# Fewer and wider small products on TensorE in a gated-DeltaNet decoder step, and another last stage

## The chip, the cores and the metric

The kernel runs on one core of a Trainium2 chip, in one launch. The metric is the device time of that launch in microseconds (us). Five engines work beside each other and wait for one another through semaphores: PE (TensorE: matmuls and transposes, results into PSUM), ACT (ScalarE), DVE (VectorE), POOL (GpSimd) and SP (SyncE, which here issues every DMA). A profile of one execution names each instruction with its engine, start, duration, output and inputs.

## What is computed

One inference step of a trunk of two layers, in fp32, over 512 prompt tokens and 64 sample tokens (8 sequences of 8 tokens), which share all weights. Layer 0 is a pooling mixer, layer 1 a gated DeltaNet mixer; each is followed by a SwiGLU feed-forward block, all with RMS norms before and after. The part that the change touches is the DeltaNet mixer and the very end:

```python
proj = h @ w_in
qkv_c, new_conv = short_conv(qkv, conv_buf, conv_w)   # width 4; conv_buf: 3 earlier rows per sample
q = l2norm(qkv_c[q part]) * 128 ** -0.5               # 8 heads of 128
k = l2norm(qkv_c[k part])                             # 8 heads of 128
v = qkv_c[v part]                                     # 16 heads of 128
o, s_new = gated_delta_chunked(q, k, v, g, beta, s0)  # exact delta rule, chunk by chunk
o = rms_norm(o, o_norm) * silu(z)
y = o @ w_out
...
x = x + rms_norm(swiglu(h, ffn_w_in[1], ffn_w_out[1]), norm_ffn_post[1])   # the last line: y_prompt, y_sample
```

`new_conv` (the last three rows before the convolution, for the prompt and for each sample) and the states are outputs too.

## The kernel before

**Layout.** Activations lie with channels on the 128 partitions and tokens along the free dimension (512 prompt columns, then 64 sample columns). Every dense product is made from three fp32r products (`mm3`): each operand is split into a high and a low part (`wh`, `wl` for weights; `hH`, `hL` or `aH`, `aL` for activations), and high times high, high times low and low times high are summed in PSUM. ACT makes the high part of a weight tile, DVE or POOL the low part (tiles `wraw`, `wh`, `wl`, three buffers each).

**The DeltaNet mixer** runs in four groups G of two key heads and four value heads. `project(G)` computes the group's eight 128-channel chunks (two of k, two of q, four of v; PSUM tile `ps_m`), convolves them on DVE and turns them to token-major by `finish`. `core(G)` computes the delta rule of the prompt (`inv32`, `scan`) and of the samples (`sample_front`, `sample_heads`). The program writes `core(G)` ahead of `project(G+1)`, and the two overlap.

The pieces that the change touches:

- *Convolution states.* For each half of a group (four chunks) the 24 stored rows (8 samples by 3) of each chunk are loaded into `crow` with 24 rows on partitions and four chunks side by side (lines 1807 to 1813), and each chunk is transposed on its own (1814, 1815). On the way out the 27 new rows of each chunk (`nct`: 3 of the prompt, 24 of the samples) are transposed one chunk at a time (1920 to 1922), copied by ACT to `nco` (which shares the one buffer of `crow`), and stored by two DMAs for each run of neighbouring chunks (1925 to 1929).
- *Norms of the samples.* The sample columns of q and k (tile `qks`, each written twice so that 128 columns are filled) are squared by DVE or POOL into `sqs` (1911, 1912). Four fp32 products with a column of ones sum the squares over the channels (1848 to 1850). The prompt's norms come from ACT squares with a running sum (`ksq`). A second product in `sample_front` brings the samples' k to token-major (`pt`, 1980), from which `ks` is made.
- *Outputs of the samples.* `TQ` holds, for two heads each, `T` in its upper 64 partitions and `Q` in partitions 64 to 127, columns 0 to 63. The output product uses one 64 by 64 corner of the array (`tile_position=(64, 64)`, 2075 to 2078). `gate_s` transposes the four heads' outputs, 64 partitions by 128 (2281 to 2287).
- *The end.* In the last block of the second feed-forward part, tokens are handled in two pieces, `LAST`: 320 and then 256 columns. Each finished chunk `yo` is squared by ACT into `nsq` and added to `nacc` (`add_sq`); `turn_y` scales it and transposes it into PSUM (`ps_B`) or, for the first four chunks of a piece, on into SBUF (`yT`). `finish1` (2454) sums `nacc` over the channels by products with ones (`ps_n`), takes the root on ACT and the reciprocal on DVE (`nrc`), and adds the scaled result to the residual (`xa`, `xb`) with four DVE instructions for the last 256 tokens, two per 128 rows. Three DMAs store these rows.

PSUM banks are used in rings (1154): `x` is one bank, through which go all transposes of `project`, `finish` and the gates; `k` has two.

**The order.** No engine runs the program in the order in which it is written. A class `Plan` records every operation, estimates its cost, places all operations with a list scheduler by priority, then moves priorities at random in windows of the schedule. The random moves to make are given by a table of seeds, `CHOSEN` (eight passes, 7,451 seeds); the operations are issued in the resulting order on each engine, SP's DMAs included. `EITHER` marks operations that the planner may give to DVE or POOL. Where PE would stand idle for long, the plan fills in products of ones (`ps_w`).

All operations are issued from two lines (785, and 781 for the fillers), so the rows of the profile are told apart by tile names.

Of the kernel before, what the change touches and what calls it, by code (L numbers as in the profile page):

```python
# [11 lines left out]
F32 = mybir.dt.float32  # L12
# [36 lines left out]
CW = 4  # L49
# [11 lines left out]
class Plan:  # L61
# [2446 lines left out]
```

## Time and profile before

| | us |
|---|---|
| three runs, median (lowest to highest) | 1501.12 (1500.25 to 1501.59) |
| the profiled execution, its own time | 1501.94 |
| the profiled execution, span from first to last instruction | 1500.2 |
| PE busy | 1476.1 |
| DVE busy | 1128.9 |
| ACT busy | 841.3 |
| POOL busy | 124.7 |

The span is shorter than the time of the same execution by 1.7 us. The DeltaNet mixer lies between 480 and 1035 us from the span's start, which is where the tiles `crow`, `nct`, `sqs`, `TQ` and `vs` appear; the last feed-forward block ends at 1489 us. A row of the timeline gives start, duration, engine, line, operation, output and inputs, and how many equal instructions are merged in it. PE's instructions overlap one another, so the slot of one product is the distance between starts, not its duration.

### The profile page before, as it was taken

How to read it: one execution, taken by the hardware profiler on the slowest of the kernel's cores; microseconds unless marked ns; L12 is line 12 of the kernel's file. 1: busy time of each engine (PE TensorE's matmuls, PEld its weight loads, DVE VectorE, ACT ScalarE, POOL GpSimd, SP SyncE). 2: the span in 40 equal slices, each digit the busy share in tenths (PEclk: the TensorE clock that was granted, in tenths of full speed). 3: DMA queues.
4: the chain of work that ended last, by engine and by line, in shares of the span. 5: the costliest groups of instructions: out<-in, count | busy, mean ns of one | idle time of the engine just before them, and what ended most of it. 6: DMA issues, size and time to landing. Idle time of an engine off the chain costs nothing.

```text
span 1500.2 us, 30095 instructions
## 1 busy us (share of the span) xinstructions
PE 1476.1 (98%) x11734; PEld 1433.4 (96%) x11734; DVE 1128.9 (75%) x2273; ACT 841.3 (56%) x1824; POOL 124.7 (8%) x258
## 2 busy tenths in 40 slices
PE   8999999999999999999999999999999999999997
PEld 8999999999999899898999899899999999999997
DVE  7994566778678797995997899567797566767855
ACT  7754443435455866865775775555474443534544
POOL 5200000000012111100220110000110000000000
PEclk9999999999999999999999999999999999999998
DMA  7643323233456433434344434746753323224162
GB/s 200 182 131 92 104 78 105 71 114 89 136 149 165 123 97 99 121 101 133 104 125 138 120 111 139 216 141 204 216 173 107 106 80 89 87 87 121 57 185 88
DMA packets 322821, 186.96 MB, mean 125 GB/s; under 512 B 13163, under 2 KB 315596, under 8 KB 322671
## 3 DMA queue, kind: packets, MB, share of 16 engines
q1 hardware_dynamic: 322679, 185.04, 42.6%
q8 instruction: 92, 1.51, 0.4%
q14 instruction: 50, 0.41, 0.1%
HBM read 154.72 MB, written 30.52 MB: 123 GB/s over the span
## 4 chain that ended last, share of the span: by engine, by line
PE 87%; DVE 7%; ACT 2%; DMA 2%; issue 1%; POOL 0%; DVEq 0%; SPq 0%; POOLq 0%; ACTq 0%
PE ps_A L785 27%; PE ps_B L785 27%; PE ps_m L785 19%; PE ps_s L785 5%; PE ps_k L785 4%; PE ps_x L785 2%; PE ps_e L785 1%; DVE wl L785 1%; DVE ac L785 1%; DVE nacc L785 1%; PE ps_n L785 1%; DMA og<-og_d 1%; DVE y L785 1%; PE ps_g L785 0%; DVE vt L785 0%
## 5 line engine op out<-in xcount | busy, mean ns | idle before, releaser
L785 ACT ACTIVATE wh<-wraw 128x1024 fp32r<-128x1024 f32 (+4 forms) x214 | 208.1, 973 | 174.8 <-PE ps_A L785 78.2
L785 DVE TENSOR_TENSOR wl<-wraw,wh 128x1024 fp32r<-128x1024 f32 (+4 forms) x214 | 238.8, 1116 | 76.4 <-ACT wh L785 70.0
L785 PE MATMUL ps_m<-hH,wh 128*128 128x320 f32 (+1 forms) x832 | 251.1, 311 | 0.0
L785 PE MATMUL ps_m<-hL,wh 128*128 128x320 f32 (+1 forms) x832 | 249.1, 308 | 0.0
L785 PE MATMUL ps_m<-hH,wl 128*128 128x320 f32 (+1 forms) x832 | 246.4, 308 | 0.0
L785 PEld LDWEIGHTS ps_m<-hH,wh 128*128 128x128 f32 x832 | 155.3, 189 | 4.8 <-issue 1.2
L785 PEld LDWEIGHTS ps_m<-hL,wh 128*128 128x128 f32 x832 | 155.3, 189 | 1.7 <-issue 0.6
L785 PEld LDWEIGHTS ps_m<-hH,wl 128*128 128x128 f32 x832 | 154.6, 189 | 1.8 <-issue 0.6
L785 PE MATMUL ps_B<-hL,wh 128*128 128x288 f32 (+2 forms) x420 | 124.1, 304 | 0.4 <-POOL hL L785 0.4
L785 PE MATMUL ps_B<-hH,wh 128*128 128x288 f32 (+2 forms) x420 | 122.8, 305 | 0.6 <-ACT hH L785 0.6
L785 PE MATMUL ps_B<-hH,wl 128*128 128x288 f32 (+2 forms) x420 | 123.1, 304 | 0.0
L785 PE MATMUL ps_A<-aL,wh 128*128 128x288 f32 (+2 forms) x408 | 116.4, 297 | 0.0
L785 PE MATMUL ps_A<-aH,wl 128*128 128x288 f32 (+2 forms) x408 | 116.0, 297 | 0.0
L785 PE MATMUL ps_A<-aH,wh 128*128 128x288 f32 (+2 forms) x408 | 115.6, 298 | 0.0
L785 PE MATMUL ps_A<-hH,wl 128*128 128x288 f32 (+2 forms) x396 | 110.4, 289 | 0.3 <-DVE wl L785 0.3
L785 PE MATMUL ps_A<-hL,wh 128*128 128x288 f32 (+2 forms) x396 | 110.3, 288 | 0.0
L785 PE MATMUL ps_A<-hH,wh 128*128 128x288 f32 (+2 forms) x396 | 110.1, 290 | 0.2 <-ACT nsq L785 0.2
L785 PE MATMUL ps_B<-aL,wh 128*128 128x288 f32 x296 | 82.9, 295 | 0.0
L785 PE MATMUL ps_B<-aH,wl 128*128 128x288 f32 x296 | 82.7, 295 | 0.0
L785 PE MATMUL ps_B<-aH,wh 128*128 128x288 f32 x296 | 82.7, 295 | 0.0
L785 DVE SCALAR_TENSOR_TENSOR ac<-u,cwt,ac 128x600 f32<-128x600 f32 x96 | 79.3, 837 | 1.5 <-ACT ac L785 1.0
L785 PEld LDWEIGHTS ps_B<-hL,wh 128*128 128x128 f32 x420 | 78.1, 188 | 0.9 <-POOL hL L785 0.9
(459 smaller groups left out, 4029.9 us busy)
## 6 DMA issues: line engine op xcount, KB each, us to landing
wraw<-in_ffn_w_in_dram SPq DMA_DIRECT2D x64, 512.0 KB
wraw<-in_gdn_w_in_dram SPq DMA_DIRECT2D x53, 512.0 KB
graw<-in_ffn_w_in_dram SPq DMA_DIRECT2D x36, 512.0 KB
wraw<-in_ffn_w_out_dram SPq DMA_DIRECT2D x26, 448.0 KB
wraw<-in_gdn_w_out_dram SPq DMA_DIRECT2D x21, 512.0 KB
wraw<-in_ffn_w_out_dram SPq DMA_DIRECT2D x32, 320.0 KB
St<-in_state_gdn_rec_dram SPq DMA_DIRECT2D x32, 256.0 KB
out_dram<-St SPq DMA_DIRECT2D x32, 256.0 KB
```

The lines of the kernel that those rows point to most:

```text
L785: calls[e](*a, **k)
```

## The change

Five edits, and a new table of seeds.

1. *Convolution states.* The rows of four chunks are stacked on 96 partitions (8 DMAs of 24 rows per group instead of 3), so that one transpose does what four did; on the way out, four chunks of 27 rows are transposed at once to 108 partitions, copied by ACT as 108 by 128 instead of 27 by 512, and stored by 16 DMAs per group instead of 6.
2. *Norms of the samples.* The products of `sqs` with ones go, and so do the squares by DVE or POOL. Instead the samples' q and k are transposed (`pt`, one per chunk, in ring `x`), and ACT squares them with a running sum into a fifth column of `ksq`. The same transpose of k gives `ks`, so that the product `pt` in `sample_front` goes; `ks` gets two buffers.
3. *Outputs of the samples.* `Q` moves to columns 64 to 127 of `TQ`, and the output product takes the whole of `TQ` and of `vn` (with zeros in its upper half, set by POOL). `gate_s` transposes all 128 partitions.
4. *The last sums.* In the last piece the square of the last chunk is no longer added to `nacc` by DVE: both tiles go through products with ones into one PSUM sum.
5. *The last adds and stores.* The pieces are taken in reverse; for the last 128 rows one half is scaled by ACT and added by POOL; and each 512-column half is stored by itself, with six DMAs instead of three.

`CHOSEN` keeps eight passes and holds 5,709 other seeds, so the order of every engine's instructions is drawn anew.

```diff
@@ out(), last block of the feed-forward part
-                add_sq(tp, s["acc"], yc, i, hf)
+                if ends and hf.i == 1 and i == NC - 1:
+                    s["acc"].append(halftile(tp, "nsq", hf, 2))
+                    ACT.activation(s["acc"][1], yc, AF.Square)
+                else:
+                    add_sq(tp, s["acc"], yc, i, hf)
@@ project()
-            sqs = pp.tile([P, 4, P], F32, name="sqs", tag="sqs", bufs=1)
+            ks = gp.tile([P, 2, P], F32R, name="ks", tag="ks", bufs=2)
...
-                crow = pp.tile([R0 + CW - 1, 4, P], F32, name="crow", tag="crow", bufs=1)[:R0]
+                crow = pp.tile([P, P], F32, name="crow", tag="crow", bufs=1)[:4 * R0]
                 for _, c, k in (r for r in runs if r[0] == j4):
                     c0 = chunks[4 * j4 + c][2] * P
-                    SP.dma_start(crow[:, c:c + k], state_gdn_conv[0].rearrange("b r d -> (b r) d")[:, c0:c0 + k * P]
-                                 .rearrange("r (c p) -> r c p", c=k))
-                for c in range(4):
-                    PE.transpose(cp[:, 4 * j4 + c], crow[:, c], ident[:R0, :R0])
+                    for i in range(k):
+                        SP.dma_start(crow[(c + i) * R0:(c + i + 1) * R0],
+                                     state_gdn_conv[0].rearrange("b r d -> (b r) d")[:, c0 + i * P:c0 + (i + 1) * P])
+                PE.transpose(cp[:, 4 * j4:4 * j4 + 4].rearrange("p c r -> p (c r)"), crow, ident[:4 * R0, :4 * R0])
@@ finish(), kind "k"
+                    pt = bank("x")[:, :P]
+                    PE.transpose(pt, qks[:, i, :2].rearrange("p x t -> p (x t)"), ident)
+                    ACT.activation(u[:, SEQ:], pt, AF.Square, accum_out=ksq[:, SPANS, i:i + 1])
+                    ACT.activation(ks[:, i], pt, AF.Copy)
+                    DVE.tensor_tensor(ks[SMP:, i], pt[SMP:], ks[SMP:, i].bitcast(F32), op=sub)
@@ finish(), kind "q"
+                    pt = bank("x")[:, :P]
+                    PE.transpose(pt, qks[:, i, 1:].rearrange("p x t -> p (x t)"), ident)
+                    ACT.activation(u[:, SEQ:], pt, AF.Square, accum_out=ksq[:, SPANS, 2 + i:3 + i])
-                        pst = bank("x")[:, :4]
-                        for c in range(4):
-                            PE.matmul(pst[:, c:c + 1], sqs[:, c], ones[:, 0:1], start=True, stop=True)
-                        DVE.tensor_scalar(vt_[:, 0, :SPANS], ksq, EPS, None, op0=add)
-                        DVE.tensor_scalar(vt_[:, 0, SPANS], pst, EPS, None, op0=add)
+                        DVE.tensor_scalar(vt_[:, 0], ksq, EPS, None, op0=add)
@@ project(), per chunk and at its end
-                if kind != "v":
-                    EITHER.tensor_tensor(sqs[:, j].rearrange("p (x t) -> p x t", x=2), dup(dss), dup(dss), op=mult)
...
-                pn_ = bank("x", (P, 4, P))[:R]
-                for c in range(4):
-                    PE.transpose(pn_[:, c], nct[:, 4 * j4 + c], ident)
-                nco = pp.tile([R, 4, P], F32, name="nco", tag="crow", bufs=1)
+                pn_ = bank("x")[:4 * R, :P]
+                PE.transpose(pn_, nct[:, 4 * j4:4 * j4 + 4].rearrange("p c r -> p (c r)"), ident)
+                nco = pp.tile([P, P], F32, name="nco", tag="crow", bufs=1)[:4 * R]
                 ACT.activation(nco, pn_, AF.Copy)
-                    for dst, src in ((nc_prompt[0, 0], nco[:CW - 1]),
-                                     (nc_sample[0].rearrange("b r d -> (b r) d"), nco[CW - 1:])):
-                        SP.dma_start(dst[:, cols].rearrange("r (c p) -> r c p", c=k), src[:, c:c + k])
+                    for i in range(k):
+                        c0, r = (chunks[4 * j4 + c][2] + i) * P, (c + i) * R
+                        SP.dma_start(nc_prompt[0, 0, :, c0:c0 + P], nco[r:r + CW - 1])
+                        SP.dma_start(nc_sample[0].rearrange("b r d -> (b r) d")[:, c0:c0 + P], nco[r + CW - 1:r + R])
@@ sample_front()
-                PE.matmul(pt, kk, ident, start=True, stop=True)
...
-                ACT.activation(ks[:, hd], pt, AF.Copy)
-                DVE.tensor_tensor(ks[E2[1], hd], pt[E2[1]], ks[E2[1], hd].bitcast(F32), op=sub)
@@ sample_heads()
+                POOL.memset(vn[lo], 0.0)
...
-                DVE.tensor_tensor(vn, pv[:, 0].rearrange("p (e v) -> p e v", e=2),
-                                  bet[:, SPANS, h2].unsqueeze(2).to_broadcast([P, 2, P]), op=mult)
+                DVE.tensor_tensor(vn[up], pv[up, 0].rearrange("p (e v) -> p e v", e=2),
+                                  bet[up, SPANS, h2].unsqueeze(2).to_broadcast([SMP, 2, P]), op=mult)
...
-                    PE.matmul(po[up, 0, e * P:(e + 1) * P], Qs[:, hd, e], vn[up, e], start=True, stop=True,
-                              tile_position=(SMP, SMP))
+                    PE.matmul(po[:, 0, e * P:(e + 1) * P], TQ[:, hd, e], vn[:, e], start=True, stop=True)
@@ gate_s()
-            po = bank("x")[:, :4 * SMP].rearrange("p (h t) -> p h t", h=4)
+            po = bank("x", (P, 4, P))
             for h in range(4):
-                PE.transpose(po[:, h], o[:, h], ident[up, up])
+                PE.transpose(po[:, h], pr_[3][:, h], ident)
@@ finish1()
+            for j, a in enumerate(acc):
+                for i, (o, n) in enumerate(PIECES[hf.i]):
+                    PE.matmul(ps[:n, i:i + 1], a[:, o - hf.o:o - hf.o + n], ones[:, 0:1], start=i + j == 0 or len(acc) == 1,
+                              stop=j + 1 == len(acc), skip_group_check=len(acc) > 1)
...
-            for i, (o, n) in enumerate(PIECES[hf.i]):
+            for i, (o, n) in reversed(list(enumerate(PIECES[hf.i]))):
...
+                    if yk.space != PSUM and hf.i == 1 and m < n:
+                        ACT.activation(yk, yk, AF.Copy, scale=r)
+                        POOL.tensor_tensor(to, to, yk, op=add)
+                    else:
+                        DVE.scalar_tensor_tensor(out=to, in0=yk, scalar=r, in1=to, op0=mult, op1=add)
+                    if hf.i == 1:
+                        cuts.append(cols)
+                for c in cuts or [slice(0, D)]:
+                    SP.dma_start(y_prompt[0, o:o + m, c], xT[o][:m, c])
+                    if m < n:
+                        SP.dma_start(y_sample.rearrange("b t d -> (b t) d")[:, c], xT[o][m:, c])
```

More of the change, by code (lines that the diff above doesn't have):

```diff
@@ L1797, in project @@
             kt = gp.tile([P, SPANS, 2, P], F32, name="kt", tag="kt", bufs=2)
-            out.append((qk, vt, qks, vs, kt))
-            ksq = pp.tile([P, SPANS, 4], F32, name="ksq", tag="ksq", bufs=1)
-            sqs = pp.tile([P, 4, P], F32, name="sqs", tag="sqs", bufs=1)
+            ks = gp.tile([P, 2, P], F32R, name="ks", tag="ks", bufs=2)
+            out.append((qk, vt, qks, vs, kt, ks))
+            ksq = pp.tile([P, SP1, 4], F32, name="ksq", tag="ksq", bufs=1)
             chunks = [("k", i, KH + 2 * G + i) for i in range(2)] + [("q", i, 2 * G + i) for i in range(2)] \
@@ L1958, in hybrid_kernel @@
         TQ = cp_.tile([P, 2, 2, P], F32, name="TQ")
-        POOL.memset(TQ[SMP:, :, :, SMP:], 0.0)
+        POOL.memset(TQ[SMP:, :, :, :SMP], 0.0)
         def sample_front(G, qks, Ts, Qs, ks):
@@ L1976, in sample_front @@
                 pkv = pk[:, :P].rearrange("p (x i) -> p x i", x=2)
-                pt = pk[:, P:2 * P]
                 kk = qks[:, hd, :2].rearrange("p x t -> p (x t)")
                 PE.matmul(pkv, kk, qks[:, hd, 1:], start=True, stop=True)
-                PE.matmul(pt, kk, ident, start=True, stop=True)
                 for e, q in enumerate(E2):
@@ L2171, in core @@
         def core(G, pr_, out):
-            qk, vt, qks, vs, kt = pr_
+            qk, vt, qks, vs, kt, ks = pr_
             QD = cp_.tile([P, 4, SPANS, P], F32, name="QD", tag="QD", bufs=1)
@@ L2176, in core @@
             out.append(oss)
-            Ts, Qs = TQ[:SMP], TQ[SMP:, :, :, :SMP]
-            ks = cp_.tile([P, 2, P], F32R, name="ks", tag="ks", bufs=1)
+            Ts, Qs = TQ[:SMP], TQ[SMP:, :, :, SMP:]
             Uv = Uw.rearrange("p (h s) i -> p h s i", h=4)
@@ L2281, in gate_s @@
         def gate_s(pr_, zss):
-            up = E2[1]
-            o = pr_[3][up]
-            po = bank("x")[:, :4 * SMP].rearrange("p (h t) -> p h t", h=4)
+            po = bank("x", (P, 4, P))
             for h in range(4):
-                PE.transpose(po[:, h], o[:, h], ident[up, up])
-            DVE.scalar_tensor_tensor(out=zss, in0=po, scalar=prm[:, G_ON:G_ON + 1], in1=zss, op0=mult, op1=mult)
+                PE.transpose(po[:, h], pr_[3][:, h], ident)
+            DVE.scalar_tensor_tensor(out=zss, in0=po[:, :, SMP:], scalar=prm[:, G_ON:G_ON + 1], in1=zss, op0=mult, op1=mult)
         def load_zs(G):
@@ L2459, in finish1 @@
             whole = hf.n // P
-            for i, (o, n) in enumerate(PIECES[hf.i]):
-                PE.matmul(ps[:n, i:i + 1], acc[0][:, o - hf.o:o - hf.o + n], ones[:, 0:1], start=True, stop=True)
+            for j, a in enumerate(acc):
+                for i, (o, n) in enumerate(PIECES[hf.i]):
+                    PE.matmul(ps[:n, i:i + 1], a[:, o - hf.o:o - hf.o + n], ones[:, 0:1], start=i + j == 0 or len(acc) == 1,
+                              stop=j + 1 == len(acc), skip_group_check=len(acc) > 1)
             for r, q in ((slice(0, P), slice(0, whole)), (slice(0, hf.n % P), slice(whole, whole + 1))):
@@ L2465, in finish1 @@
                     DVE.reciprocal(rc[r, q], rc[r, q])
-            for i, (o, n) in enumerate(PIECES[hf.i]):
+            for i, (o, n) in reversed(list(enumerate(PIECES[hf.i]))):
+                m = min(n, SEQ - o)
+                cuts = []
                 for k in range(2):
-                    to = xT[o][:, k * 4 * P:(k + 1) * 4 * P]
-                    DVE.scalar_tensor_tensor(out=to, in0=yT[o, k], scalar=rc[:n, i:i + 1], in1=to, op0=mult, op1=add)
-                m = min(n, SEQ - o)
-                SP.dma_start(y_prompt[0, o:o + m], xT[o][:m])
-                if m < n:
-                    SP.dma_start(y_sample.rearrange("b t d -> (b t) d"), xT[o][m:])
+                    cols = slice(k * 4 * P, (k + 1) * 4 * P)
+                    to, yk, r = xT[o][:, cols], yT[o, k], rc[:n, i:i + 1]
+                    if yk.space != PSUM and hf.i == 1 and m < n:
[9 more added lines that the diff above has]
+                        SP.dma_start(y_sample.rearrange("b t d -> (b t) d")[:, c], xT[o][m:, c])
         ffn(1, x, y, wts, xp, ap_, tp, 3, HALVES, finish1, turn_x(), turn_y)
```

1 line of the change is left out of this document (removed), and 798 rows, old and new, of the table CHOSEN.

## The prediction

> **What bounds the kernel now.** I read the page's busy times first, then the chain that ended last.
>
> ```profile
> PE 1476.1 (98%) x11734; PEld 1433.4 (96%) x11734; DVE 1128.9 (75%) x2273; ACT 841.3 (56%) x1824; POOL 124.7 (8%) x258
> ...
> PE 87%; DVE 7%; ACT 2%; DMA 2%; issue 1%; POOL 0%; DVEq 0%; SPq 0%; POOLq 0%; ACTq 0%
> ```
>
> PE is without work for only 1500.2 - 1476.1 = 24.1 us, and 87% of the chain lies on it. But a share over the whole span could hide stages with another limit, so I asked for the busy time by stage. Edits 1 to 3 lie between 480 and 1035 us. Columns: stretch, sum, then PE, PEld, DVE, ACT, POOL, clock, DMA share, GB/s.
>
> ```profile
> 680.00:780.00 100.00, 97.74 (x891) 90.93 (x890) 80.83 (x200) 70.20 (x212) 21.10 (x38) 1.00 0.44 125
> 780.00:880.00 100.00, 99.56 (x911) 92.45 (x910) 83.44 (x209) 64.90 (x201) 12.42 (x30) 1.00 0.46 130
> 880.00:950.00 70.00, 67.09 (x626) 65.28 (x625) 60.67 (x152) 44.69 (x100) 6.04 (x14) 1.00 0.47 139
> ```
>
> PE is idle 2.3, 0.4 and 2.9 us in these, DVE 17 to 19 us per 100 and ACT 30 to 35, at full clock. So PE bounds the mixer too, and a slot that it no longer spends shortens the stage, until DVE's or ACT's chain ends last. The stretch from 880 us is the weakest: the last group has no projection beside it.
>
> **The price of a slot.** PE's products overlap, so I do not take their durations (0.27 us for a transpose) but the distance between starts. PE's own timeline gives it, with the neighbours' slots taken off.
>
> ```profile
> 516.42 0.31 PE L785 MATMUL ps_m<-hH,wl 128*128 128x320 f32 x1
> 516.56 0.31 PE L785 MATMUL ps_m<-hH,wh 128*128 128x320 f32 x1
> 516.71 0.94 PE L785 MATMUL ps_x<-ones,sqs 128*128 128x1 f32 x8
> 517.52 0.39 PE L785 MATMUL ps_m<-hL,wh 128*128 128x320 f32 x1
> 517.75 0.31 PE L785 MATMUL ps_m<-hH,wl 128*128 128x320 f32 x1
> ```
>
> A plain product of 320 columns takes 516.56 - 516.42 = 0.145 us (by columns, 256 take about 0.117). From 516.56 to 517.75 there are 1.19 us for two of them and eight records of `sqs`: (1.19 - 0.29) / 8 = 0.112 us a record. An fp32 product leaves two records, so the four products with one column cost 0.90 us per group.
>
> ```profile
> 682.07 0.31 PE L785 MATMUL ps_m<-hL,wh 128*128 128x320 f32 x1
> 682.21 0.60 PE L785 MATMUL ps_x<-ident,nct 128*27 128x128 f32 x4
> 682.57 0.39 PE L785 MATMUL ps_m<-hH,wl 128*128 128x320 f32 x1
> 682.80 0.31 PE L785 MATMUL ps_m<-hH,wh 128*128 128x320 f32 x1
> ```
>
> Four transposes of `nct`: 0.73 - 0.29 = 0.44 us, 0.11 each. A transpose is one record, and its 27 or 128 stationary columns do not show in the slot.
>
> ```profile
> 481.82 0.31 PE L785 MATMUL ps_m<-hH,wh 128*128 128x320 f32 x1
> 482.06 0.42 PE L785 MATMUL ps_x<-ident,crow 24*128 24x24 f32 x4
> 482.42 0.39 PE L785 MATMUL ps_m<-hH,wh 128*128 128x256 f32 x1
> 482.64 0.42 PE L785 MATMUL ps_m<-hL,wh 128*128 128x256 f32 x2
> ```
>
> Four transposes of `crow` with 24 rows: 0.82 - 0.145 - 0.117 = 0.56 us, though they stream only 24 columns. A gap of 0.09 us stands ahead of the first, and the product behind them starts late: going into the small form and out again costs more than the work.
>
> ```profile
> 864.83 0.30 PE L785 MATMUL ps_m<-hH,wh 128*128 128x320 f32 x1
> 865.06 0.65 PE L785 MATMUL ps_s<-sn,TQ 64*64 64x128 f32 x4
> 865.64 0.41 PE L785 MATMUL ps_m<-hL,wh 128*128 128x320 f32 x1
> 865.89 0.28 PE L785 MATMUL ps_s<-vH,km 128*128 128x256 f32 x1
> ```
>
> The output products of one key head (two, so four records) in the 64 by 64 corner: 1.06 - 0.29 = 0.77 us.
>
> **The change part by part**, over four groups:
>
> - *States in* (8 halves): 0.56 us goes, one transpose of 96 rows comes. The trace has no 96-row form; it is not above a 128-row one (0.11) unless it also pays the passage of the 24-row form (then 0.11 + 0.34 = 0.45). I take 0.11, nearest in rows: 8 x 0.45 = **-3.6 us** (-0.9 to -4.0).
> - *States out*: 32 transposes become 8 of the same streamed length: 24 x 0.11 = **-2.6 us**.
> - *Norms*: 32 records of `sqs` go, 32 x 0.112 = -3.6 us. The product that made `pt` (two records, eight times: 16 x 0.112 = 1.8) goes, and 16 transposes of 0.11 come (1.8): **-3.6 us** together.
> - *Outputs*: 8 x (0.77 - 4 x 0.112) = **-2.6 us** if the full array is paid at the slot of other full 128-column records; zero if the corner's price was all in its neighbours.
> - *Gates*: four times four transposes leave a 64-row form. The corner's gain of 0.32 per passage bounds it: -1.3 to 0, I take **-0.6 us**.
>
> That is -13.0 us of PE slots. In the Trainium skill, "TensorEngine Tiling (Array Packing)", sections "Overview" and "Key Properties", a product small in both dimensions is said to gain up to 2x from smaller tiles, and changing the tiling mode is said to drain the engine. The second agrees with the 0.56 us above; the first speaks against edit 3, and is a rival below.
>
> What hides the rest of it:
>
> ```profile
> L785 ACT ACTIVATE u<-ps_x 128x128 f32<-128x128 f32 x32 | 8.5, 284 | 0.1
> ...
> L785 ACT ACTIVATE nco<-ps_x 27x512 f32<-27x512 f32 x8 | 4.7, 586 | 9.4 <-DMA out_dram<-nco 7.0 <-PE ps_x L785 2.4
> ```
>
> ACT gets 16 squares of 0.28 us, at most doubled by reading the accumulator (4.5 to 9 us over four groups), and loses half of each `nco` copy (8 x 0.29 = 2.3). Net 2 to 7 us, against 30 us of idle time per 100: hidden. The two copies and subtractions for `ks` only move from bank ring `k` to `x`, ahead of the core that needs them. DVE and POOL lose the squares; POOL gets eight small memsets at 9 to 21% busy. If that cover were gone, the 7 us would be paid. SP issues 15 more DMAs per group, behind one buffer: the `nco` row shows ACT waiting 7.0 us for earlier stores. I cost that at nothing, since PE's idle time beside it is 7 us at most in the mixer's stages shown; the third rival prices it.
>
> PE's order is drawn anew. What a drawn order leaves idle in the three stretches is 0.4 to 2.9 us each; I allow 3 us either way. And since the last group's stretch is idle for 2.9 us already, I take 1 us off the gain there: **-12.0 us** from edits 1 to 3.
>
> **The end.** Timeline of all engines, weight loads left out:
>
> ```profile
> 1489.83 0.40 ACT L785 ACTIVATE nsq<-yo 128x256 f32<-128x256 f32 x1
> ...
> 1490.26 0.42 DVE L785 TENSOR_TENSOR nacc<-nacc,nsq 128x256 f32<-128x256 f32 x1 [0.70 <-ACT nsq L785]
> ...
> 1490.85 0.56 PE L785 MATMUL ps_n<-ones,nacc 128*128 128x1 f32 x4
> ...
> 1491.94 0.75 DVE L785 SCALAR_TENSOR_TENSOR xb<-yT,nrc,xb 128x512 f32<-128x512 f32 x1
> ...
> 1493.38 1.11 SPq L785 DMA_DIRECT2D out_dram<-xb  x2
> 1493.93 0.74 DVE L785 SCALAR_TENSOR_TENSOR xa<-yT,nrc,xa 128x512 f32<-128x512 f32 x1
> 1494.70 0.42 SPq L785 DMA_DIRECT2D out_dram<-xa  x1
> ```
>
> The square ends at 1490.23. Without the add, the products with ones start a hop later (the 0.17 us from 1490.68 to 1490.85), at 1490.40: 0.45 us earlier. The products of the old `nacc` lie under the wait for the square. The first add then starts near 1491.5; four adds have starts 0.66 us apart (1.99 / 3), three end 0.66 us sooner, near 1493.55. POOL's path is one scaling on ACT (about the 0.6 us of its 512-column copies above) and one add:
>
> ```profile
> L785 POOL TENSOR_TENSOR vt<-vt,oss 128x512 f32<-128x512 f32 x4 | 4.6, 1166 | 3.4 <-DVE oss L785 3.4
> ```
>
> 1491.5 + 0.6 + 1.17 is 1493.3: not late. The stores: the first can be issued after the first half, near 1492.25 instead of 1493.38, 1.1 us earlier. Six issues at 0.42 to 0.56 us take until about 1495.2, as late as before, but the last one moves 128 KB and not 512.
>
> ```profile
> 1498.00:1498.50 0.50, 0.00 (x0) 0.00 (x0) 0.00 (x0) 0.00 (x0) 0.00 (x0) 0.50 0.37 148
> ```
>
> Bytes flow until about 1498.5, 5.1 us after the first issue, for 1 MB in all (256 rows of 4 KB): if that flow sets the end, it moves with the first issue, **-1.1 us**. If the issues set it, the last 128 KB (under 1 us by that flow) end up to 2.2 us sooner; if nothing but order changes, 0.
>
> The Trainium skill, "SBUF — State Buffer", section "Who interferes with whom", says that a DVE instruction with two SBUF inputs and a GpSimd instruction that reads SBUF shut each other out. One of DVE's three remaining adds has both inputs in SBUF; by that rule an add of 0.66 us comes behind POOL's, and the end gains 0.4 instead of 1.1. No row here shows the two together, so the sum goes without it.
>
> **The sum.** -12.0 - 1.1 = -13.1 us. The profiled execution's span goes from 1500.2 to 1487.1 and its time, 1.7 us above the span, from 1501.9 to 1488.8. The median of the runs is 0.8 us lower: **1488.0 us**. Own range: high with states in at their dear bound (+2.7), the corner's gain at half (+1.3), nothing at the end (+1.1) and 1 us of a worse order, 1494; low with 3 us of a better order, the end at -2.2 and the gates at -1.3, 1482.
>
> **The rivals.**
>
> 1. *DVE's and ACT's chains take over.* DVE is 81 to 87% busy here, and parts of each group are serial. For: the 2.3 and 2.9 us of idle PE show that it happens already. Against: 0.4 us in 780 to 880. If half of the 13 us becomes waiting: 1501.1 - 6.5 - 1.1 = 1493.5 us.
> 2. *No change.* PE's slots go, but the mixer ends when the chains do: only the end is left, 1500 us.
> 3. *Slower: the one buffer of `crow` and `nco`.* Each `nco` half now needs 8 stores instead of 2 or 4, each at about 0.3 us on SP, and the next half waits for the last. ACT, in order, stands with weight splits queued behind it, and SP with the next weight loads. The tile's own view gives SP's time for an issue (shortest, median, longest, ns):
>
> ```profile
> L785 SPq DMA_DIRECT2D out_dram<-nco x24: 258/302/541, 564.0 to 949.7; - x24
> ```
>
> Price: today 7.0 / 8 = 0.9 us a copy; with 6 x 0.3 us more, 2.7, eight times for stores and as much again for loads, 43 us. It decides once over a third of that reaches PE, which eats the gain; at 17 us the time is 1501.1 - 13.1 + 17 = 1505 us. Against: of the 7.0 us today little can have reached PE, which was idle for 0.4 us in a whole group's stretch.
> 4. *The full array is dearer than the corner.* If the smaller tile did halve the price, the eight output pairs would cost 2 x 0.77 each, +6.2 us instead of -2.6: 1496.8 us. Against: the full 128-column records at 0.112.
>
> **How the numbers follow.** Forecast 65%, first rival 20%, second 8%, third 5%, fourth 2%. About 0.2%, 3 us, is what a measurement can tell from no change: below 1498.1 lie the forecast and rivals 1 and 4, 87%; within lies rival 2, 8%; above lies rival 3, 5%. The range reaches over the first rival with some room, 1482 to 1496; outside remain rivals 2 to 4 and the forecast's tails.
>
> **What would show it.** PE's busy time near 1464 us, with the idle time still near 24; eight records each of `crow` and `nct`, none of `sqs`, 16 transposes of `qks` in `ps_x`, and `TQ` without a 64*64 form; the first add 1.7 us after the last square's start (2.1 before), three adds on DVE, last bytes 1 us sooner behind it. Idle PE above 30 us means rival 1 or 3: 3 if ACT's idle time ahead of `nco` is over 20 us, 1 if PE waits for DVE's `rs`, `vn` or `QD`. A 96-row transpose with a gap before it would refute the first term; an unchanged busy PE, the whole argument.

## The result, and the profile after

The changed kernel takes **1491.28 us** (median of six runs, 1489.17 to 1492.77) against 1501.37 us (1500.25 to 1503.11) for the one before: a ratio of 0.9931, 95% interval 0.9919 to 0.9944, or 10.1 us less. The forecast was 1488.0 us, the range 1482 to 1496.

The profiled execution took 1492.77 us with a span of 1491.0 us, so the spans differ by 9.2 us. The changed kernel's page, busy times and then the chain that ended last:

```profile
PE 1466.2 (98%) x11638; PEld 1425.8 (96%) x11638; DVE 1127.1 (76%) x2263; ACT 845.7 (57%) x1858; POOL 110.6 (7%) x255
...
PE 60%; issue 27%; DVE 8%; DMA 2%; ACT 2%; POOL 1%; POOLq 0%; SPq 0%; ACTq 0%; DVEq 0%
```

PE's busy time falls by 9.9 us (1476.1 to 1466.2) and its idle time stays (24.1 to 1491.0 - 1466.2 = 24.8 us): PE is still the bound. Not all of the 9.9 us is work of the edits. The new order also holds 82 fillers `ps_w` instead of 102, none of them in the mixer; with the fillers left out, the records of both traces give 1463.5 and 1454.9 us, 8.5 us less. ACT gained 4.4 us of work, as costed (2 to 7). The chain's share on PE fell from 87 to 60% and "issue" rose from 1 to 27%; with PE's idle time as it was, I read that as another path through the same back-to-back work and not as a new limit; no run tests this reading.

By stage, from starts and ends in PE's timeline of both traces:

| from one mark to the next | before, us | after, us | difference |
|---|---|---|---|
| start to the first projection product of the mixer (`ps_e`) | 449.4 | 450.0 | +0.6 |
| to the last gate transpose (`vs`) | 583.7 | 574.9 | -8.8 |
| to the first transpose of `x` behind the output projection | 54.2 | 54.6 | +0.5 |
| to the last product of the second feed-forward part | 401.9 | 401.9 | 0.0 |
| to the end of the span | 11.1 | 9.6 | -1.5 |

One trace of each kernel does not fix these lengths to tenths. Three runs below issue the changed kernel's mixer without any change, and by the same marks theirs take 574.9, 574.9 and 573.0 us; so the mixer gained 8.8 to 10.7 us. The first stage takes 449.0 to 450.2 us in three traces with the order of before, so its +0.6 is not shown to be a loss.

**What PE saved.** The removed and the new transposes and products, in the tile views of the changed kernel (shortest, median and longest duration in ns, first and last start, form):

```profile
L685 PE MATMUL ps_x<-ident,crow x8: 246/248/277, 483.6 to 832.8; 96*128 96x96 f32 x8
...
L685 PE MATMUL ps_x<-ident,nct x8: 271/276/291, 557.3 to 931.1; 128*108 128x128 f32 x8
...
L685 PE MATMUL ps_x<-ident,qks x16: 270/272/328, 495.2 to 859.5; 128*128 128x128 f32 x16
...
L685 PE MATMUL ps_s<-sn,TQ x32: 270/275/347, 601.5 to 991.2; 128*128 128x128 f32 x32
```

The counts are those forecast. The slots are read from distances between starts again, in PE's timeline of the changed kernel:

```profile
713.92 0.31 PE L685 MATMUL ps_m<-hH,wh 128*128 128x320 f32 x1
714.07 0.25 PE L685 MATMUL ps_x<-ident,crow 96*128 96x96 f32 x1
714.10 0.36 PE L685 MATMUL ps_m<-hH,wl 128*128 128x256 f32 x1
714.30 0.28 PE L685 MATMUL ps_s<-vH,km 128*128 128x256 f32 x1
...
974.02 0.31 PE L685 MATMUL ps_m<-hL,wh 128*128 128x320 f32 x1
974.17 0.60 PE L685 MATMUL ps_s<-sn,TQ 128*128 128x128 f32 x4
974.53 0.39 PE L685 MATMUL ps_m<-hH,wh 128*128 128x320 f32 x1
974.76 0.31 PE L685 MATMUL ps_m<-hH,wl 128*128 128x320 f32 x1
```

From 713.92 to 714.30 stand a product of 320 columns (0.145), the new transpose and a product of 256 (0.117): 0.12 us for the transpose, and no gap ahead of it, so a 96-row form doesn't pay the passage that the 24-row one paid. From 974.02 to 974.76 stand two products and four records of `TQ`: (0.74 - 0.29) / 4 = 0.112 us each, against 0.77 us per four in the corner. Both prices are nearly as forecast (0.11 and 0.112). But what *went* was smaller than eight times the groups that I had priced, because small forms often stood next to each other. PE's timeline of the kernel before:

```profile
721.24 0.31 PE L785 MATMUL ps_m<-hL,wh 128*128 128x320 f32 x1
721.48 0.42 PE L785 MATMUL ps_x<-ident,crow 24*128 24x24 f32 x4
721.83 0.65 PE L785 MATMUL ps_s<-sn,TQ 64*64 64x128 f32 x4
722.41 0.41 PE L785 MATMUL ps_m<-hH,wl 128*128 128x320 f32 x1
722.66 0.28 PE L785 MATMUL ps_s<-vH,km 128*128 128x256 f32 x1
```

From 721.24 to 722.66 are 1.42 us; less two products, 1.13 us for both groups, where 0.56 + 0.77 = 1.33 was the sum of the prices: one passage is shared. Added up over every group of both traces, with the late start of the product behind counted to the group: `crow` 4.00 to 1.05, `nct` 3.74 to 0.98, norms (with `pt`) 5.51 to 1.95, outputs 5.95 to 3.74, gates 2.14 to 1.80. Together **-11.8 us**, where -13.0 was forecast.

**What came back.** The mixer of this trace is 8.8 us shorter, not 11.8 (10.7 shorter in the best of the four). Windows over the whole mixer (stretch, sum, then PE, PEld, DVE, ACT, POOL, clock, DMA share, GB/s), first the kernel before, then the changed one:

```profile
480.00:1050.00 570.00, 562.82 (x4867) 527.97 (x4866) 456.46 (x1110) 376.10 (x1038) 70.55 (x144) 1.00 0.46 131
```

```profile
480.00:1050.00 570.00, 561.32 (x4851) 529.30 (x4850) 459.67 (x1103) 380.69 (x1073) 61.47 (x145) 1.00 0.47 135
```

PE's idle time there rose from 7.2 to 8.7 us in this trace. In the three others with the same mixer it is 7.1 to 7.8 us, so most of what is missing is no idle time that the profile shows. It lies in the slots of products that the change leaves alone; other neighbours, or waits too short to empty PE, could be the cause, and no run separates them. The wait view of PE over this stretch begins with these pairs (us in total, times, longest). `QD` is not new (1.6 us, three times, before); `zz` and `BD` are:

```profile
PE ps_m L685 <- ACT zz L685: 2.1, 1, 2.1
PE ps_k L685 <- DVE QD L685: 2.0, 4, 0.7
PE ps_k L685 <- DVE BD L685: 1.5, 1, 1.5
```

The third rival's buffer is not among them here, but it is in other traces. PE waited for the copy `nco` in the kernel before, and again in three of the four traces with the changed mixer. First the kernel before, then the second run of the changed kernel (2.4 and 2.5 us in the other two):

```profile
PE ps_x L785 <- ACT nco L785: 1.7, 1, 1.7
```

```profile
PE ps_x L685 <- ACT nco L685: 2.8, 1, 2.8
```

The tile view of `nco` of the changed kernel, in the first trace:

```profile
L685 ACT ACTIVATE nco<-ps_x x8: 258/278/282, 557.8 to 937.7; 108x128 f32<-108x128 f32 x8
...
  DMA out_dram<-nco: 0.9, 1
```

There are 64 stores now instead of 24, and ACT waited 0.9 us for them, once, where it had waited 7.0 (0.5 to 3.5 us in the three other traces). So the buffer cost PE about 1 us more than before, far from the 43 us that the third rival priced.

**The end**, timeline of all engines of the changed kernel:

```profile
1482.07 0.40 ACT L685 ACTIVATE nsq<-yo 128x256 f32<-128x256 f32 x1
1482.53 0.60 PE L685 MATMUL ps_n<-ones,nsq 128*128 128x1 f32 x4
...
1483.73 0.75 DVE L685 SCALAR_TENSOR_TENSOR xb<-ps_B,nrc,xb 128x512 f32<-128x512 f32 x1
1484.40 0.74 DVE L685 SCALAR_TENSOR_TENSOR xa<-yT,nrc,xa 128x512 f32<-128x512 f32 x1
1484.46 1.80 POOL L685 TENSOR_TENSOR xb<-xb,yT 128x512 f32<-128x512 f32 x1 [381.17 <-ACT yT L685]
1484.51 1.11 SPq L685 DMA_DIRECT2D out_dram<-xb  x2
1485.06 0.75 DVE L685 SCALAR_TENSOR_TENSOR xa<-ps_B,nrc,xa 128x512 f32<-128x512 f32 x1
1485.72 1.02 SPq L685 DMA_DIRECT2D out_dram<-xa  x2
1486.84 1.11 SPq L685 DMA_DIRECT2D out_dram<-xb  x2
```

The first add starts 1.66 us after the last square (1.7 forecast, 2.11 before), the first store 2.44 us after it (3.55 before), and the span ends 1491.0 - 1482.1 = 8.9 us after it (10.4 before). POOL's add took 1.80 us and not 1.17. The changed kernel with the first four passes of its seeds (below) has another order here: POOL begins when the add with two inputs in SBUF is done, beside adds that read PSUM, and takes 1.27 us.

```profile
1483.34 0.75 DVE L685 SCALAR_TENSOR_TENSOR xa<-yT,nrc,xa 128x512 f32<-128x512 f32 x1
1484.14 1.27 POOL L685 TENSOR_TENSOR xb<-xb,yT 128x512 f32<-128x512 f32 x1 [380.39 <-ACT yT L685]
```

The length of the end varies too. Five traces with the very same end, issued at the same distances from the square to 0.02 us, take 8.8 to 9.3 us from the square; before, three traces take 10.4 and one 10.7.

### The profile page after: what moved, and what is told of

Its sections match the earlier page's. It is cut to its first block, busy times and chain, and to the rows that moved or that the text cites. A ratio compares the mean times of both kernels' runs of the same rounds, so it can differ in the third digit from the quotient of the medians.

```text
span 1491.0 us, 30006 instructions
## 1 busy us (share of the span) xinstructions
PE 1466.2 (98%) x11638; PEld 1425.8 (96%) x11638; DVE 1127.1 (76%) x2263; ACT 845.7 (57%) x1858; POOL 110.6 (7%) x255
## 4 chain that ended last, share of the span: by engine, by line
PE 60%; issue 27%; DVE 8%; DMA 2%; ACT 2%; POOL 1%; POOLq 0%; SPq 0%; ACTq 0%; DVEq 0%
PE ps_m L685 18%; PE ps_B L685 16%; PE ps_A L685 13%; PE ps_k L685 4%; PE ps_s L685 4%; PE ps_x L685 2%; PE ps_e L685 1%; DVE ac L685 1%; DVE wl L685 1%; DMA og<-og_d 1%; DVE y L685 1%; PE ps_n L685 0%; PE ps_g L685 0%; DVE nacc L685 0%; DVE Uw L685 0%
```

## The experiments

Two things had to be told apart: whether PE's slots made the gain, or what else was redrawn with them; and what of the end earned its 1.5 us. Each run was made from the changed kernel or from the one before by changing what is issued at a place, with every other instruction left in its order, unless said otherwise.

**The changed kernel again**, five executions, timed with the next three:

> The changed kernel itself, as the mark for the three others on the same chip. All theories: 1491 us, within 1.5 us.

1490.92 us, ratio 0.9938 (0.9924 to 0.9951). This is the number that the next three are compared with.

**The old forms of PE's work, in the new order.** Four 24-row transposes ahead of each transpose of `crow`, each transpose of `nct` four times, the eight one-column records per group, the corner, the 64-row gates; everything else as in the changed kernel.

```diff
@@ issued at the places of the new forms
+ def four(real): 4 x transpose(cp[:, 4 * j4], crow[:R0], ident[:R0, :R0]); real()
+ norms: 4 x matmul(px[:, 500 + c:501 + c], ident, ones[:, 0:1]) where j == 3
+ nct:   real() four times
+ out:   matmul(po[up, ...], Qs[:, hd, e], vn[up, e], tile_position=(64, 64))
+ gates: transpose(po[:, h, 64:], pr_[3][64:, h], ident[64:, 64:])
```

> PE's old small forms are issued again at the places of the new ones, in the changed kernel's own order on every engine. Slot theory (the mixer is as long as PE's slots, so edits 1 to 3 earned the sum of their slots, 11.8 us by the two traces, and the missing 2 to 3 us are the new order): +12.8 us against the changed kernel (four passages of 24 rows more per half 4.0, three more transposes of nct per half 2.6, eight one-column records per group 3.7, corner for full array 2.2, gates 0.3), so about 1504 us, PE busy +12 us. Chain theory (DVE's and ACT's chains set the stage, slots are half hidden): +6 us or less, PE's idle time falls by what is hidden.

```profile
PE 1479.2 (99%) x11726; PEld 1434.4 (96%) x11726; DVE 1128.5 (75%) x2263; ACT 846.2 (56%) x1858; POOL 111.6 (7%) x255
```

1501.69 us, ratio 1.0013 (1.0005 to 1.0022). By its page (above) PE is busy for 1479.2 us, 12.4 more than in the run again (1466.8), and the time is 10.8 us longer: some 85% of the slots come out as time. That is near the 12.8 of the slots and far from the 6 at most of the chains. The mixer takes 585.5 us in the trace, 10.6 more than in the run again, so the time is lost where the old forms stand. DVE, ACT and POOL do the work of the changed kernel here, so their edits did not make the gain.

It also shows something that was not asked. This run has the end's edits (-1.5 us), and eight 96-row transposes too many (+1.05), and is still 1.7 us above the kernel before, whose PE work it does. So the new order, with the other engines' edits, is about 1.7 + 1.5 - 1.05 = 2.2 us worse for the old forms than the old order.

**One edit of PE back at a time.** The corner alone, then the 24-row transposes alone.

```diff
- matmul(po[:, 0, e * P:(e + 1) * P], TQ[:, hd, e], vn[:, e])
+ matmul(po[up, 0, e * P:(e + 1) * P], Qs[:, hd, e], vn[up, e], tile_position=(64, 64))
```

> Only the samples' output product goes back to the 64 by 64 corner, in the changed kernel's order. Slot theory with passages: 5.95 us for the corner's 32 records against 3.74 in the full array, +2.2 us. Smaller-tile rule (a tile of half the rows and columns is up to twice as fast): -1.9 us. Chain theory: within 0.5 us of the changed kernel.

```diff
+ 4 x transpose(cp[:, 4 * j4], crow[:R0], ident[:R0, :R0])   # ahead of the 96-row transpose
```

> Four transposes of 24 rows are put ahead of each of the eight transposes of crow, all else as in the changed kernel. Slot theory with passages (0.56 us a group of four): +4.0 to +4.5 us. If only the records counted and the passage were hidden: +2.8 us. Chain theory: +2 us or less.

The tile views of these two, first the run with the corner, then the one with the 24-row transposes:

```profile
L1989 PE MATMUL ps_s<-sn,TQ x32: 269/269/320, 602.2 to 991.9; 64*64 64x128 f32 x32
```

```profile
L1732 PE MATMUL ps_x<-ident,crow x32: 213/215/238, 483.5 to 837.1; 24*128 24x24 f32 x32
...
L692 PE MATMUL ps_x<-ident,crow x8: 301/303/308, 483.9 to 837.3; 96*128 96x96 f32 x8
```

The corner gives 1492.76 us, ratio 0.9951 (0.9938 to 0.9963), 1.8 us above the run again (2.2 expected; by the rival of the cheaper tile it would have been 1.9 below). The spans of the two profiled executions, though, are 1491.0 and 1490.9 us, and their mixers 575.3 and 574.9. A corner record takes 0.269 us by duration, a full one 0.270 to 0.275: the durations agree, and only the passage around the group differs. The small transposes give 1493.61 us, 0.9963 (0.9951 to 0.9976), 2.7 us above, where 4.0 to 4.5 was expected with the passages and 2.8 without. Their slots grew by 3.8 us in the trace, PE's busy time by 2.6. So the passages are there in the slots, but a third did not reach the time, which came out as the second expectation has it. The interval of the corner's run overlaps that of the run again: that the corner is not cheaper by 1.9 us is shown, but how much dearer it is in time is not settled.

**Fewer passes of the drawn order.** The table of seeds cut to its first pass, and to its first four, for both kernels.

```diff
-        for chosen in self.CHOSEN:
+        for chosen in self.CHOSEN[:1]:      # and [:4]
```

> The kernel before, its order refined by the first of its eight passes of seeds only. Order theory (the time is the slots of the edits plus what the drawn order leaves idle, and that differs from table to table by some us): the plan's own estimate of its length is 7.3 us above that of all eight passes, so about 1507 us.

> The changed kernel with the first of its passes only. Order theory: the plan's estimate is 11.3 us above that of all eight, so about 1502 us, and the same edits earn only some 5 to 8 us against the kernel before with one pass. Rival, that the edits alone decide and an order is as good as another with equal passes: 10 us apart, as with eight passes.

> The kernel before with the first four of its passes. Order theory: the plan's estimate is 3.1 us above that of eight, about 1503 us.

> The changed kernel with the first four of its passes. Order theory: the plan's estimate is 3.3 us above that of eight, about 1494 us, 9 to 11 us below the kernel before with four passes. Rival: also 10 us apart, so this pair alone tells nothing; with the pair of one pass it does.

| passes | before, us | after, us | after less before | mixer before and after, one trace each |
|---|---|---|---|---|
| one | 1516.46 (ratio 1.0102, 1.0084 to 1.0121) | 1499.34 (0.9996, 0.9988 to 1.0005) | -17.1 | 586.0 and 575.7: -10.3 |
| four | 1504.59 (1.0033, 1.0022 to 1.0044) | 1491.81 (0.9945, 0.9932 to 0.9958) | -12.8 | 583.9 and 573.2: -10.7 |
| eight | 1500.03 | 1491.28 (other runs: 1490.92) | -9 to -10 | 583.7 and 573.0 to 574.9: -8.8 to -10.7 |

The pages of the two kernels with one pass, before and after:

```profile
PE 1488.4 (98%) x11756; PEld 1441.0 (95%) x11756; DVE 1127.4 (74%) x2284; ACT 838.1 (55%) x1826; POOL 116.3 (8%) x247
```

```profile
PE 1475.3 (98%) x11658; PEld 1433.2 (96%) x11658; DVE 1124.7 (75%) x2263; ACT 840.5 (56%) x1856; POOL 109.8 (7%) x255
```

PE's busy time differs by 13.1 us here, 2.9 of them fillers (124 and 102). The times lie 17.1 us apart, more than the slots explain, and both expectations for one pass were missed. The last column shows where the difference does not come from: in the mixer, where edits 1 to 3 lie, the gain is about the same under all three tables. The rest lies in the end and in stages that no edit touches but that are drawn anew with everything else; and the six executions of the kernel before with one pass reach from 1510.2 to 1519.3 us (the profiled one has a span of 1513.3, against 1499.1 after). So the two kernels as wholes differ by 9 to 17 us, by the drawing, but edits 1 to 3 earn 9 to 11 us under each. The order theory, which expected only 5 to 8 us for one pass, is refuted either way. The kernel before gained 4.6 us from its last four passes, the changed one about half a us.

**The end: the fourth add on DVE.** One execution. ACT's scaling and POOL's add go, DVE makes the fourth add.

```diff
- ACT.activation(yk, yk, AF.Copy, scale=r); POOL.tensor_tensor(to, to, yk, op=add)
+ DVE.scalar_tensor_tensor(out=to, in0=yk, scalar=r, in1=to, op0=mult, op1=add)
```

> The changed kernel, but the fourth of the last adds is done by DVE in the place of ACT's scaling and POOL's add. Read from the start of the last square to the end of the span, which is 8.9 us in the changed kernel and 10.4 before. If taking an add off DVE is what shortened the end (a term of 0.66 us): 9.5 us or more. If POOL, which took 1.80 us beside DVE's add from SBUF, is no faster than a fourth add on DVE, and SP's row of issues ends as late either way: 8.9 us, within 0.2.

Timeline of that run, from the last square:

```profile
1482.11 0.40 ACT L694 ACTIVATE nsq<-yo 128x256 f32<-128x256 f32 x1
...
1485.09 0.74 DVE L2385 SCALAR_TENSOR_TENSOR xb<-yT,nrc,xb 128x512 f32<-128x512 f32 x1
1485.75 1.11 SPq L694 DMA_DIRECT2D out_dram<-xa  x2
1485.76 0.74 DVE L694 SCALAR_TENSOR_TENSOR xa<-ps_B,nrc,xa 128x512 f32<-128x512 f32 x1
1486.92 1.12 SPq L694 DMA_DIRECT2D out_dram<-xb  x2
```

The last DVE add ends at 1486.50 and the last stores are issued at 1486.92, 4.81 us after the square against 4.77 with POOL, 0.04 us later. The span of 1490.8 us ends 8.7 us after the square, against 8.9. The second engine earned nothing that shows in a spread of 8.8 to 9.3 us.

**The end: whole rows.** One execution, with three stores instead of six.

```diff
- for c in cuts: dma_start(y_prompt[0, o:o + m, c], xT[o][:m, c]); ...
+ dma_start(y_prompt[0, o:o + m], xT[o][:m]); ...     # behind the second half only
```

> The changed kernel, but the last 256 rows are stored whole, by three DMAs, each at the place of the second halves' stores. Read from the start of the last square to the end of the span. If the end is the first issue plus the flow of 1 MB: the first issue comes 1.3 us later, so 10.2 us. If it is the last issue plus a fixed latency: the last issue starts earlier than in the changed kernel, but moves 256 to 512 KB, 8.9 us or less.

Timeline of that run:

```profile
1479.96 0.40 ACT L694 ACTIVATE nsq<-yo 128x256 f32<-128x256 f32 x1
...
1483.72 0.34 SPq L2391 DMA_DIRECT2D out_dram<-xa  x1
1484.18 0.48 SPq L2394 DMA_DIRECT2D out_dram<-xb  x1
1484.70 0.66 SPq L2391 DMA_DIRECT2D out_dram<-xb  x1
```

Here the first store is issued 3.76 us after the square, 1.3 us later than with halves, and the span of 1489.5 us ends 9.5 us after it: 0.6 us later, between the expectations. By this one execution halves are worth 0.6 us, half of what their first issue gains. But 9.5 is only 0.2 above the longest of the five traces of the same end with halves, so the size is not settled.

**The edits in the order of before.** The last two runs were to show what the new order costs by leaving it away: the kernel before, with edits 1 to 3 issued at the places of the operations that they replace, and then the end's edits too (without POOL's add).

```diff
- 4 x transpose(cp[:, 4 * j4 + c], crow[:, c], ident[:R0, :R0])
+ transpose(cp[:, 4 * j4:4 * j4 + 4], crowf[:4 * R0, 0], ident[:4 * R0, :4 * R0])   # at the place of the fourth
- 4 x transpose(pn_[:, c], nct[:, 4 * j4 + c], ident)
+ transpose(pnf[:4 * R, 0], nct[:, 4 * j4:4 * j4 + 4], ident)                       # at the place of the fourth
- 4 x matmul(pst[:, c:c + 1], sqs[:, c], ones[:, 0:1])
+ 4 x transpose(psf[:, c], qks[:, ...], ident)
+ 4 x ACT.activation(sqs[:, c], psf[:, c], AF.Square, accum_out=vt_[:, 1, SPANS, c:c + 1])
...
```

> The kernel before with edits 1 to 3 put in at the place of the operations that they replace, so that every engine keeps the order of before; the end stays as it was. One difference to the change: the product that makes ks stays where it is, as a transpose, so that 8 transposes more (0.9 us) are left than in the change. By the slots read from the two traces PE loses 5.7 (states) + 2.9 (norms) + 2.2 (outputs) + 0.3 (gates) = 11.1 us. Theory 'the drawn order took some 3 us back': here nothing is drawn, so all of the 11.1, or 85% of them as the run with the old forms put back counted them, come out: 1490.3 to 1492. Rival 'the loss lies in the edits themselves (ACT's squares, more stores, more waits on ring x), whatever the order': the loss of 3 us stays, and the end's 1.4 us are missing: 1493.5 to 1495.

> The same with the end's edits in the order of before: the last square summed by products of its own, the stores of the last 256 rows in halves, but all four adds on DVE. Theory 'the drawn order took some 3 us back': 1.1 us below the run with edits 1 to 3 alone, 1489 to 1491, so that it is at or below the changed kernel (1491.2) although it drew nothing. Rival 'the loss lies in the edits themselves': 1492 to 1494, above the changed kernel.

The window over the mixer, then DVE's wait view, of the first run; the third fence is the same wait in the kernel before:

```profile
480.00:1050.00 570.00, 555.33 (x4756) 517.82 (x4755) 452.46 (x1095) 374.81 (x1065) 64.06 (x141) 1.00 0.46 129
```

```profile
DVE rv L1880 <- ACT sqs L1879: 5.9, 4, 2.4
```

```profile
DVE rv L785 <- PE ps_x L785: 0.7, 1, 0.7
```

1506.27 us (ratio 1.0044, 1.0030 to 1.0058) and 1507.11 us (1.0037, 1.0025 to 1.0050): slower than before, and both expectations are refuted. PE's slots went (some 9 us of the 11.1 planned, counted as above), but PE idles 570.0 - 555.3 = 14.7 us in the mixer where the kernel before idles 7.2, and the other products' slots add up to 6.7 us more. The order worked out for the long work did not fit the short one as I put it in. One delay can be seen: the norms' squares now stand between the transposes and DVE's `rv`, so that DVE waits four times, 5.9 us in all, where it waited 0.7. It is not shown to be a cause, for the changed kernel has nearly the same wait and is 15 us faster:

```profile
DVE rv L685 <- ACT u L685: 4.6, 2, 4.0
```

How much of the loss lies in such places of mine, and how much in the order as a whole, these runs don't separate. The second run's end is 9.4 us long from the square (10.7 in the first): that part of the edits helps in either order. In it the first add starts 2.06 us after the square although the sum is made in PSUM as in the change (2.12 in the first run), so the end was shortened there without an earlier first add. That the second run is slower all the same comes from the stages which the two runs share: they are 2.5 us longer in its trace.

## Why the prediction was right, and where it was not

*The marks.* PE's busy time near 1464 us with idle time near 24: 1466.2 and 24.8, though 1.4 us of the fall are fillers, of which the prediction says nothing. Counts of `crow`, `nct`, `qks` and `TQ`, three adds on DVE, the first add after 1.7 us: as said.

*PE bounds the kernel, and a slot saved is time saved.* Right, with a condition that I had not seen. Back in the new order, the old forms cost 10.8 us of time for 12.4 us of busy PE. But in the order of before, some 9 us of slots went and the time rose by 5.6 us. Under the three drawn tables the slots came out as 9 to 11 us of mixer. So a slot was worth its time where the order was drawn for it; whether another hand-made order would also have kept it is not shown.

*Durations don't price a slot; the distance of starts does.* Right: 0.12 us for a 96-row transpose and 0.112 per full record came out as forecast, and 0.269 us of duration in the corner would have promised nothing.

*States in* (-3.6): -2.95; *outputs* (-2.6): -2.2; *gates* (-0.6): -0.3. The step that was mis-sized: I priced one group of each kind, between two plain products, and multiplied by eight. Groups that stand together share a passage, as the rows at 721 us show. *States out* (-2.6): -2.75, *norms* (-3.6): -3.56, both right.

*Smaller tiles.* The Trainium skill, "TensorEngine Tiling (Array Packing)", section "Overview", splits the array into several independent tiles and gives a speedup of up to 2x for a dimension of 64 or less. Read as a promise for edit 3's product, which used one tile at a time, that rule did not hold here: the corner's 32 records cost 5.95 us of slots against 3.74 in the full array, and no time was gained by going back to it. The Trainium skill, same page, section "Key Properties", says that changing the tiling mode drains the engine; the gaps at 721 us agree, where the first `crow` transpose starts 0.24 us after a product whose slot is 0.145.

*What hides the rest.* Right in the main: ACT's 4.4 us, the copies of `ks` and the 60 added DMAs of the states found room. The third rival (stores behind one buffer) did not come: 0.5 to 3.5 us of waiting where 20 was its mark. But the term that I put at nothing is about 1 us: PE waited for `nco` for 2.4 to 2.8 us in three of four traces, 1.7 before.

*1 us off for the last group, and ±3 us for the order.* Edits 1 to 3 were to earn 12.0 us; of 11.8 us of slots 8.8 to 10.7 reached the mixer's length. The 1 to 3 us that are missing did not come as the forecast has it: PE's idle time in the mixer is 7.1 to 8.7 us, 7.2 before, so at most 1.5 us of them are waiting that the profile shows, and the cause of the rest stays open. The time of 1491.3 us lies between the first rival's 1493.5 and the forecast's 1488.0, but DVE's and ACT's chains are not shown to have made the difference. The cut tables move the two kernels as wholes by several us, more than my 3, in stages that the edits don't touch. A slip of the prediction's range: 3 us of a better order, 1.1 more at the end and 0.7 more at the gates come to 1483, not 1482.

*The end* (-1.1): -1.5, and that the size came near is partly luck, for the steps did not add up as I had them. The first add did start 0.45 us sooner (1.66 us after the square, 2.11 before), but the same sum in PSUM in the order of before moved it by only 0.06, so the new order has a part in it. The third add instead of the fourth (0.66 us) gave nothing: the run with four adds on DVE ends no later. By the run with whole rows, the first store, issued 1.3 us sooner, gave 0.6 of it, with traces of one and the same end up to 0.6 us apart. How the 1.5 us divide among the sum, the halves and the pieces' order, which was not tried alone, stays open. The rule of the Trainium skill, "SBUF — State Buffer", "Who interferes with whom", agrees with the traces: POOL's add took 1.80 us while DVE's add of two SBUF inputs ran from 1484.40 to 1485.14, and 1.27 us in the trace where the two do not meet. The add that was delayed was POOL's; I had worked it out with DVE's add behind POOL's. It cost nothing here: POOL's add ended at 1486.26, and SP was busy with the issues of the other stores until 1486.74.

**What stays open:** what takes the 1 to 3 us between slots and mixer, how the end's 1.5 us divide, and why the edits lose time in the order of before. Four passes and eight give the changed kernel nearly the same time, so more passes of this kind are not likely to return much.

## What to carry to other kernels

Price a small product by the distance of starts around it, and over all its places, since small forms that stand together share the passage that makes it dear. Where the order of instructions is worked out for one program, an edit and its order are one change: time the old work in the new order and the new work in the old, and do not add an edit's slots to an order that stays. When a new order moves the whole program, read what an edit is worth from its own stage, and from more than one trace of the same instructions. At the end of a kernel, find out which work the last store waits for before giving part of it to a second engine.

## What the runs showed of the hardware

A transpose of 96 rows has no gap ahead of it and costs 0.12 us, where four of 24 rows cost 0.56 between plain products, or about 0.2 less beside another small form. The four records of an output product cost 0.77 us alone in the 64 by 64 corner and 0.45 in the full array, at nearly the same durations. POOL's 512-column add took 1.80 us beside a DVE instruction with both inputs in SBUF, and 1.27 beside DVE instructions that read PSUM. And the time from the last square to the end of the span varied from 8.8 to 9.3 us between traces in which the end's adds and stores were issued at the same distances from that square, to 0.02 us.
